# A raw weight block in tile 1's last products and 256-column halves in tile 0's, at the two boundaries of a one-core transformer layer

## Chip, cores and metric

The kernel runs on one core of one Trainium2 chip. The metric is the device time of one execution in microseconds (us). The engines are PE (TensorE, matrix products; PEld is its weight loading), DVE (VectorE), ACT (ScalarE), POOL (GpSimd) and SP (SyncE, which here only issues transfers).

## What is computed

One layer on 256 tokens of width 2048: a feed-forward block, a token mixer and a second feed-forward block, each fed by a layer norm modulated with a shift and a scale (adaLN), and each followed by a gated, scaled residual and another layer norm. All in float32.

```python
def _modulate(x, shift, scale):
    return _layernorm(x) * (1 + scale) + shift

def _swiglu(h, w_in, w_out):
    gate, up = jnp.split(h @ w_in, 2, axis=-1)
    return (jax.nn.silu(gate) * up) @ w_out

def _layer(x, c, w_ada, b_ada, ...):
    ada = (jax.nn.silu(c) @ w_ada + b_ada)[:, None, :]
    sh1, sc1, g1, sh2, sc2, g2, sh3, sc3, g3 = jnp.split(ada, N_ADA, axis=-1)
    h = _swiglu(_modulate(x, sh1, sc1), ffn1_w_in, ffn1_w_out)
    x = _layernorm(ALPHA * x + 0.5 * (1 + g1) * h, ln1_g, ln1_b)
    h = _token_mixer(_modulate(x, sh2, sc2), w_in, ..., w_out)
    x = _layernorm(ALPHA * x + (1 + g2) * h, ln2_g, ln2_b)
    h = _swiglu(_modulate(x, sh3, sc3), ffn2_w_in, ffn2_w_out)
    x = _layernorm(ALPHA * x + 0.5 * (1 + g3) * h, ln3_g, ln3_b)
    return x
```

The inner width of the feed-forward blocks is 5632, that of the mixer 2048.

## The kernel before

**Products.** The 256 tokens are two tiles of 128, called tile 0 and tile 1 (the index `a`). A float32 operand is split into a high part in the format fp32r and the low rest (`split`, line 131: ACT casts the high part, DVE subtracts). A product is then three PE instructions, high x high, high x low and low x high (`mm3`, line 359). Where the unsplit float32 values are multiplied instead (line 604), one product of 512 columns shows as two PE instructions.

**Weights.** `load_w` (line 348) loads 1 MB from SP's queue into one of three buffers `raw`; the parts go to six buffers `hi` and six `lo`. The adaLN weights `ar` stream beside this, 512 KB at a time, through two buffers `araw`. Each is multiplied by the conditioning and accumulated on DVE (lines 145 and 147). A call `npump()` after a block of weights asks for the next of them; `need(n)` asks for all up to a point.

**Output projections.** `out_proj` (line 389) runs three times: after the first feed-forward block, after the mixer and after the second feed-forward block. It goes over column groups of 1024, 512 and 512. In the last group a block of weights has 4 rows of 128 and 512 columns. The last three blocks (`nheld`) are held: their products are kept back and issued by `finish`, first all of tile 0 (36 PE instructions), then all of tile 1 (36). The block ahead of them, like all earlier ones, is multiplied for both tiles as it arrives (24 instructions).

**Boundaries.** `boundary` (line 509) follows the first and the second projection. On DVE its order is written out by hand: tile 0's `add_up` (gate, residual, statistics: lines 420, 422, 425), `row_std`, the affine step of the layer norm in parts (`ln_affine`, lines 472 and 477, with a square and its sum on ACT for each part, line 482), the statistics of the result (`ln_stats`, lines 488 to 503), then the normalised rows `n` (line 319 on DVE, 321 on ACT), which PE transposes (line 325). The first step of tile 1's `add_up` stands inside tile 0's `ln_stats`, its other two behind the first `n`. Once transposed and modulated, tile 0 is multiplied with three raw blocks of the next weights (`cols_1024`, line 604), and then tile 1. The third projection ends in `to_out` (line 568), which adds up, normalises and stores.

**Order.** Inside the boundary, DVE's instructions keep the order of the code. Otherwise a planner puts each engine's instructions in order; a buffer goes to whoever asked for it first in the code.

Of the kernel before, what the change touches and what calls it, by code (L numbers as in the profile page):

```python
# [15 lines left out]
P = 128  # L16
# [18 lines left out]
def layer_kernel(  # L35
# [312 lines left out]
    def load_w(src, nk, w, name):  # L348
# [3 lines left out]
        for q in range(nk // h):  # L352
# [3 lines left out]
            for kk in range(h):  # L356
                yield q * h + kk, hi[:, kk, :], lo[:, kk, :]

    def mm3(o, ah, al, bh, bl, start, stop):
        PE.matmul(o, ah, bh, start=start, stop=False)  # L360
        PE.matmul(o, ah, bl, start=False, stop=False)  # L361
        PE.matmul(o, al, bh, start=False, stop=stop)  # L362
# [25 lines left out]

    def out_proj(w, rows, nk, tag, npump, finish, before=None, turn=0, nheld=3):
        st = [stat_tile(f"{tag}{a}") for a in range(2)]  # L390
# [10 lines left out]
        for width in (1024, 512, 512):  # L401
# [3 lines left out]
            lastg = col + width == D  # L405
            held = []

            def products(a, args):
                ts_ = slice(a * P, (a + 1) * P)
                for k, hh, hl, hi, lo in args:  # L410
                    for b in range(nb):
                        mm3(ps[a, b], hh[:, ts_], hl[:, ts_], hi[:, b * 512:(b + 1) * 512],
                            lo[:, b * 512:(b + 1) * 512], k == turn, k == (turn - 1) % nk)


            def add_up(a, ps=ps, col=col, bs=range(nb)):
                for b in bs:
                    cs = slice(col + b * 512, col + (b + 1) * 512)
                    r = res[:, a, cs]
                    V.tensor_tensor(out=ps[a, b], in0=ps[a, b], in1=gate[:, cs], op=ALU.mult)  # L420
                    yield
                    V.scalar_tensor_tensor(out=r, in0=r, scalar=ALPHA, in1=ps[a, b],
                                           op0=ALU.mult, op1=ALU.add)
                    yield
                    V.bn_stats(st[a][:, col // 512 + b, :], r)
                    yield

            for i in range(nu):
                u = (i + turn // kn) % nu
                hs = []  # L430
                if before:
                    before(u * kn)
                for k in range(u * kn, u * kn + kn, 2):
                    hs += rows(k)
                for kk, hi, lo in load_w(w[u * kn * P:(u + 1) * kn * P, col:col + width], kn, width,
                                         f"{tag}o{col}_{u}"):
                    arg = (u * kn + kk, *hs[kk], hi, lo)
                    if lastg and i >= nu - nheld or not lastg and i == nu - 1:
                        held.append(arg)
                    else:  # L440
                        for a in range(2):
                            products(a, [arg])
                if not lastg and i == nu - 1:

                    late += [add_up(a, bs=(b,)) for b in range(nb) for a in range(2)]
                    products(0, held)
                    catch_up(2)
                    products(1, held)
                else:
                    catch_up(2)  # L450
                if not lastg or i < nu - 4:
                    npump()
            if lastg:
                catch_up(99)
                finish(lambda a: products(a, held), add_up, st)
            else:
# [11 lines left out]
    def ln_affine(a, rs, mv, lgb, sums, tag):  # L468
        for h in range(2):
# [4 lines left out]
            yield  # L474
        for i, (c0, c1) in enumerate(((0, 1024), (1024, 1536), (1536, 2048))):
            r = res[:, a, c0:c1]
            V.scalar_tensor_tensor(out=r, in0=r, scalar=rs, in1=lgb[1][:, c0:c1], op0=ALU.mult, op1=ALU.add,
                                   accum_out=sums[:, i:i + 1])
            if i == 0:
                V.tensor_scalar_mul(sums[:, 4:5], sums[:, 0:1], -2.0 / D)  # L480
            sq = npool.tile([P, 1024], F32, tag="sq", name=f"sq_{tag}{a}{i}")
# [4 lines left out]
    def ln_stats(out_, sums, tag):  # L486
# [4 lines left out]
        yield  # L491
        V.tensor_scalar(out=s[3], in0=s[1], scalar1=s[0], scalar2=1.0 / D, op0=ALU.subtract, op1=ALU.mult)
        yield
        V.tensor_scalar(out=s[2], in0=s[3], scalar1=s[3], scalar2=-1.0, op0=ALU.mult, op1=ALU.mult)
        yield
# [13 lines left out]
    def boundary(products, add_up, st, lgb, v, tag, xT, entry, nk):  # L509
# [3 lines left out]
        with tc.manual_schedule(engines={mybir.EngineType.DVE}):  # L513
            products(0)
            products(1)
            for _ in add_up(0):
                pass
# [5 lines left out]
            together(lns[0])  # L523
            up = add_up(1)
            next(up)
            together(lns[0])
# [4 lines left out]
            next(m0[1])  # L531
            next(up)
            next(up, 0)
            together(row_std(mv[1], rs[1], st[1], f"{tag}a1"))
# [33 lines left out]
    def to_out(products, add_up, st, lgb):  # L568
        mv, rs = ([small(n, t, f"{t}_last{a}") for a in range(2)] for n, t in ((2, "mv"), (1, "rs")))
        with tc.manual_schedule(engines={mybir.EngineType.DVE}):  # L570
            products(0)
            products(1)
            def first(a, j):
# [9 lines left out]
            for a in range(2):  # L583
                for _ in add_up(a):
                    pass
# [227 lines left out]

    out_proj(ffn1_w_out[0], h_rows, KF, "f1", at(R_OUT), finish1)
    xp, npool = ent["xp"], ent["np"]
# [385 lines left out]

    out_proj(w_out[0], y_rows, KD, "mx", step, finish2, before, 4, 3)
    xp, npool = ent["xp"], ent["np"]
# [115 lines left out]
```

## Time and profile before

| what | value |
|---|---|
| median of 3 runs | 1977.12 us (1975.76 to 1977.9) |
| the profiled execution's own time | 1974.53 us |
| its span, first to last instruction | 1972.8 us |
| mean granted PE clock | 0.991 |
| tile 0's add-up begins, boundary 1 and 2 | 778.70 and 1208.08 us |
| first transposition, boundary 1 and 2 | 792.03 and 1221.52 us |
| tile 1's add-up begins in `to_out` | 1960.09 us |

The profile is of one execution. Its lines give an engine, the line of the kernel, the operation, the tiles written and read, and times in us (a mean or the shortest, median and longest in ns). Idle time stands in brackets with what ended it. The profiled execution is 2.6 us under the median of the runs.

### The profile page before, as it was taken

The numbers are of one execution on the slowest core, as the hardware profiler recorded it, in microseconds if no ns is written. First come the engines' busy times: TensorE is split into PE (matmuls) and PEld (weight loads), VectorE is DVE, ScalarE is ACT, GpSimd is POOL, SyncE is SP. The second block draws the span as 40 slices with busy tenths as digits, with TensorE's granted clock in tenths as the row PEclk, the third lists the DMA queues.
The fourth block names the chain that finished last, engine by engine and source line by source line (L and its number), as shares of the span: only waits on it lengthen the run. The fifth ranks groups of instructions, "written<-read, shape, count | busy, mean of one in ns | idle before, by whom it ended". The sixth has DMA issues, their size and how long they took to land.

```text
span 1972.8 us, 32259 instructions
## 1 busy us (share of the span) xinstructions
PE 1899.0 (96%) x13057; PEld 1730.9 (88%) x13057; DVE 1494.4 (76%) x1878; ACT 962.5 (49%) x1394; POOL 5.7 (0%) x17
## 2 busy tenths in 40 slices
PE   3999999999999999999999998999999999999997
PEld 3999999999988887588899876898999999988886
DVE  7798888777778897678788689678757645555776
ACT  3644454443444555645655544655444444444553
POOL 0000000000000000000000000000000000000000
PEclk9999999999999999999999999999999999999998
DMA  9998878989989785489887875898858755665552
GB/s 332 337 331 312 300 242 288 311 293 305 304 298 324 262 303 195 140 304 307 257 294 261 281 263 179 259 309 298 266 193 276 257 193 193 227 200 192 192 192 85
DMA packets 301820, 510.89 MB, mean 259 GB/s; under 512 B 10818, under 2 KB 158690, under 8 KB 300648
## 3 DMA queue, kind: packets, MB, share of 16 engines
q1 hardware_dynamic: 300808, 505.70, 76.0%
q0 software_dynamic: 864, 3.15, 0.5%
q8 instruction: 102, 1.67, 0.3%
q14 instruction: 46, 0.38, 0.1%
HBM read 506.71 MB, written 2.10 MB: 258 GB/s over the span
## 4 chain that ended last, share of the span: by engine, by line
PE 77%; DVE 9%; DMA 8%; ACT 2%; issue 2%; DVEq 0%; SPq 0%; ACTq 0%
PE o_f L360 8%; PE o_f L362 8%; PE o_f L361 8%; PE gu_f L362 8%; PE gu_f L360 8%; PE gu_f L361 8%; DMA ar<-in_w_ada_dram 5%; PE s L362 3%; PE s L360 3%; PE s L361 3%; DVE acc L147 2%; PE fs L362 1%; PE fs L360 1%; PE fs L361 1%; PE fh L362 1%
## 5 line engine op out<-in xcount | busy, mean ns | idle before, releaser
L147 DVE SCALAR_TENSOR_TENSOR acc<-ar,csil,acc 128x1024 f32<-128x1024 f32 x242 | 307.9, 1273 | 109.5 <-DMA ar<-in_w_ada_dram 108.1
L360 PE MATMUL s<-xhi_f,hi_s 128*128 128x256 f32 x768 | 215.0, 280 | 0.7 <-ACT hi_s L132 0.6
L362 PE MATMUL s<-xhi_f,lo_s 128*128 128x256 f32 x768 | 214.3, 280 | 0.3 <-DVE lo_s L133 0.3
L361 PE MATMUL s<-xlo_f,hi_s 128*128 128x256 f32 x768 | 214.5, 279 | 0.0
L362 PE MATMUL gu_f<-xhi_f,lo_f2i 128*128 128x256 f32 x768 | 212.3, 276 | 0.0
L360 PE MATMUL gu_f<-xhi_f,hi_f2i 128*128 128x256 f32 x768 | 212.3, 276 | 0.0
L361 PE MATMUL gu_f<-xlo_f,hi_f2i 128*128 128x256 f32 x768 | 212.3, 276 | 0.0
L133 DVE TENSOR_TENSOR lo_f2i<-raw_f2i,hi_f2i 128x1024 fp32r<-128x1024 f32 x96 | 117.3, 1224 | 88.9 <-ACT hi_f2i L132 88.9
L360 PE MATMUL gu_f<-xhi_f,hi_f1i 128*128 128x256 f32 x640 | 177.1, 277 | 0.3 <-DVE hT L727 0.3
L362 PE MATMUL gu_f<-xhi_f,lo_f1i 128*128 128x256 f32 x640 | 177.0, 277 | 0.0
L361 PE MATMUL gu_f<-xlo_f,hi_f1i 128*128 128x256 f32 x640 | 176.9, 276 | 0.0
L132 ACT CAST hi_f2i<-raw_f2i 128x1024 fp32r<-128x1024 f32 x96 | 100.6, 1049 | 132.1 <-PE gu_f L361 115.7
L132 ACT CAST hh<-hT 128x512 fp32r<-128x512 f32 x130 | 80.1, 623 | 141.0 <-PE o_f L361 138.2
L360 PEld LDWEIGHTS s<-xhi_f,hi_s 128*128 128x128 f32 x768 | 146.2, 191 | 1.0 <-ACT hi_s L132 0.7
L362 PEld LDWEIGHTS s<-xhi_f,lo_s 128*128 128x128 f32 x768 | 145.8, 190 | 0.8 <-DVE lo_s L133 0.8
L361 PEld LDWEIGHTS s<-xlo_f,hi_s 128*128 128x128 f32 x768 | 146.3, 190 | 0.3 <-DVE xlo_f L309 0.3
L361 PEld LDWEIGHTS gu_f<-xlo_f,hi_f2i 128*128 128x128 f32 x768 | 144.3, 188 | 0.2
L360 PEld LDWEIGHTS gu_f<-xhi_f,hi_f2i 128*128 128x128 f32 x768 | 144.2, 188 | 0.2
L362 PEld LDWEIGHTS gu_f<-xhi_f,lo_f2i 128*128 128x128 f32 x768 | 144.2, 188 | 0.0
L132 ACT CAST hi_s<-raw_s 128x1024 fp32r<-128x1024 f32 x96 | 97.4, 1050 | 95.5 <-DMA raw_s<-in_ffn_w_in_dram 56.3
L133 DVE TENSOR_TENSOR lo_f2o<-raw_f2o,hi_f2o 128x1024 fp32r<-128x1024 f32 x88 | 107.8, 1225 | 44.9 <-ACT hi_f2o L132 44.8
L360 PE MATMUL o_f<-hi_f2o,hh 128*128 128x512 f32 x344 | 135.3, 393 | 0.0
(451 smaller groups left out, 5373.3 us busy)
## 6 DMA issues: line engine op xcount, KB each, us to landing
ar<-in_w_ada_dram SPq DMA_DIRECT2D x288, 512.0 KB, 5.6
raw_s<-in_ffn_w_in_dram SPq DMA_DIRECT2D x48, 1024.0 KB, 6.3
raw_f2i<-in_ffn_w_in_dram SPq DMA_DIRECT2D x48, 1024.0 KB, 5.1
raw_f1o<-in_ffn_w_out_dram SPq DMA_DIRECT2D x44, 1024.0 KB, 7.0
raw_f2o<-in_ffn_w_out_dram SPq DMA_DIRECT2D x44, 1024.0 KB, 5.1
raw_f1i<-in_ffn_w_in_dram SPq DMA_DIRECT2D x40, 1024.0 KB, 7.4
raw_mxo<-in_w_out_dram SPq DMA_DIRECT2D x16, 1024.0 KB, 5.6
raw_fh<-in_ffn_w_in_dram SPq DMA_DIRECT2D x16, 1024.0 KB, 6.8
```

The lines of the kernel that those rows point to most:

```text
L132: S.copy(hi, src)
L133: V.tensor_tensor(out=lo, in0=src, in1=hi.bitcast(F32), op=ALU.subtract)
L147: V.scalar_tensor_tensor(out=acc, in0=raw, scalar=csil[:, k:k + 1], in1=acc, op0=ALU.mult, op1=ALU.add)
L360: PE.matmul(o, ah, bh, start=start, stop=False)
L361: PE.matmul(o, ah, bl, start=False, stop=False)
L362: PE.matmul(o, al, bh, start=False, stop=stop)
```

## The change

- `load_kept` loads the block ahead of the held ones by two transfers of 512 KB into the two `araw` buffers, and splits each. It is used in the first and the second projection (`raw_row`). This block's products for tile 0 are issued as it arrives; those for tile 1 come at the head of tile 1's last products, as unsplit float32 values (`hT` or `yF` times the raw weights), four products of 512 columns.
- `products` can go by columns of a given width. Tile 0's held products go by 256 columns at all three places, tile 1's only in `to_out`. `add_up` can do the same: tile 0's at the boundaries, and both tiles' in `to_out`.
- The affine step's last parts are 512, 768 and 768 columns instead of 1024, 512 and 512. The estimate of the mean comes from the first part, so the constants of `ln_stats` change with it.
- At the boundaries, all of tile 1's `add_up` comes behind the first two `n`.

```diff
+    def load_kept(src, nk, w, name):
+        h = nk // 2
+        for q in range(2):
+            raw = ap.tile([P, h, w], F32, tag="araw", bufs=2, name=f"raw_{name}{q}")
+            SP.dma_start(raw, src[q * h * P:(q + 1) * h * P].rearrange("(k p) n -> p k n", p=P))
+            hi = wp.tile([P, h, w], F32R, tag="hi", bufs=6, name=f"hi_{name}{q}")
+            lo = wp.tile([P, h, w], F32R, tag="lo", bufs=6, name=f"lo_{name}{q}")
+            split(raw, hi, lo)
+            for kk in range(h):
+                yield q * h + kk, hi[:, kk, :], lo[:, kk, :], raw[:, kk, :]
...
-            def products(a, args):
+            def products(a, args, w=512):
                 ts_ = slice(a * P, (a + 1) * P)
-                for k, hh, hl, hi, lo in args:
-                    for b in range(nb):
-                        mm3(ps[a, b], hh[:, ts_], hl[:, ts_], hi[:, b * 512:(b + 1) * 512],
-                            lo[:, b * 512:(b + 1) * 512], k == turn, k == (turn - 1) % nk)
+                for c in range(0, 512, w):
+                    for k, hh, hl, hi, lo in args:
+                        for b in range(nb):
+                            bs = slice(b * 512 + c, b * 512 + c + w)
+                            mm3(ps[a, b][:, c:c + w], hh[:, ts_], hl[:, ts_], hi[:, bs], lo[:, bs],
+                                k == turn, k == (turn - 1) % nk and c + w == 512)
+
+            def last_products(a, w=512):
+                if a:
+                    for k, raw in kept:
+                        PE.matmul(ps[1, 0], raw_row(k)[:, P:], raw, start=k == turn, stop=False)
+                products(a, held, w)
...
+                keep = lastg and i == nu - nheld - 1 and raw_row
+                for kk, hi, lo, *raw in (load_kept if keep else load_w)(
+                        w[u * kn * P:(u + 1) * kn * P, col:col + width], kn, width, f"{tag}o{col}_{u}"):
                     arg = (u * kn + kk, *hs[kk], hi, lo)
-                    if lastg and i >= nu - nheld or not lastg and i == nu - 1:
+                    if keep:
+                        products(0, [arg])
+                        kept.append((u * kn + kk, raw[0]))
+                    elif lastg and i >= nu - nheld or not lastg and i == nu - 1:
                         held.append(arg)
...
-        for i, (c0, c1) in enumerate(((0, 1024), (1024, 1536), (1536, 2048))):
+        for i, (c0, c1) in enumerate(((0, 512), (512, 1280), (1280, 2048))):
...
-                V.tensor_scalar_mul(sums[:, 4:5], sums[:, 0:1], -2.0 / D)
+                V.tensor_scalar_mul(sums[:, 4:5], sums[:, 0:1], -4.0 / D)
...
-            products(0)
+            products(0, 256)
             products(1)
-            for _ in add_up(0):
+            for _ in add_up(0, w=256):
                 pass
...
             together(lns[0])
-            up = add_up(1)
-            next(up)
             together(lns[0])
...
             next(m0[0])
             next(m0[1])
-            next(up)
-            next(up, 0)
+            for _ in add_up(1):
+                pass
...
-            products(0)
-            products(1)
+            products(0, 256)
+            products(1, 256)
...
-                for _ in add_up(a):
+                for _ in add_up(a, w=256):
                     pass
...
-    out_proj(ffn1_w_out[0], h_rows, KF, "f1", at(R_OUT), finish1)
+    out_proj(ffn1_w_out[0], h_rows, KF, "f1", at(R_OUT), finish1, raw_row=lambda k: hT[:, k, :])
...
-    out_proj(w_out[0], y_rows, KD, "mx", step, finish2, before, 4, 3)
+    out_proj(w_out[0], y_rows, KD, "mx", step, finish2, before, 4, 3, lambda k: yF[:, k, :])
```

31 lines of the change are left out of this document (15 added, 16 removed).

## The prediction

> **What bounds the kernel now.** I read the page first: busy times, then the chain that ended last.
> ```profile
> PE 1899.0 (96%) x13057; PEld 1730.9 (88%) x13057; DVE 1494.4 (76%) x1878; ACT 962.5 (49%) x1394; POOL 5.7 (0%) x17
> ...
> PE 77%; DVE 9%; DMA 8%; ACT 2%; issue 2%; DVEq 0%; SPq 0%; ACTq 0%
> ```
> PE is busy for 96% of the span, so an edit pays only where PE idles or where its work shrinks. Of the places that this edit touches, two are such idles. I read the timeline there, engine by engine (columns: start us, length us, engine, line, operation, and in brackets the idle time before it with its releaser). Boundary 1:
> ```profile
> 778.70 0.70 DVE L420 TENSOR_TENSOR o_f<-o_f,gate 128x512 f32<-128x512 f32 x1 [4.97 <-PE o_f L362]
> ...
> 784.51 1.28 DVE L477 SCALAR_TENSOR_TENSOR res<-res,rs,lb 128x1024 f32<-128x1024 f32 x1 [0.42 <-ACT rs L264]
> ...
> 785.91 0.74 DVE L477 SCALAR_TENSOR_TENSOR res<-res,rs,lb 128x512 f32<-128x512 f32 x1
> 786.03 1.15 ACT L482 ACTIVATE sq<-res,sums 128x1024 f32<-128x1024 f32 x1 [1.55 <-DVE sums L480]
> 788.78 0.19 ACT L482 ACTIVATION_READ_ACCUMULATOR sq<-res,sums 128x1 f32 x1
> 788.26 0.69 DVE L420 TENSOR_TENSOR o_f<-o_f,gate 128x512 f32<-128x512 f32 x1
> 789.00 0.27 DVE L498 TENSOR_SCALAR sums<-sums 128x1 f32<-128x1 f32 x1
> 791.48 0.41 DVE L319 TENSOR_SCALAR n<-res,mr 128x256 f32<-128x256 f32 x1
> 792.03 1.09 PE L325 MATMUL tp<-ident,n 128*128 128x128 f32 x4 [5.13 <-DVE n L319]
> 804.63 1.09 ACT L321 ACTIVATE n<-res,mr 128x256 f32<-128x256 f32 x2 [2.58 <-DVE mr L503]
> 806.35 0.60 PE L325 MATMUL tp<-ident,n 128*128 128x128 f32 x4
> ```
> Tile 0's last product ends at 778.7. DVE then runs the layer norm, 12.8 us up to `n` at 791.48. PE works on tile 1's products meanwhile and then waits 5.13 us for the first transposition (792.03). Tile 1's own chain gives its `n` at 804.63 (the first of the pair is ready near 805.2), yet its transposition comes only at 806.35: there PE was late, by 1.1 us. Boundary 2 is the same code:
> ```profile
> 1208.08 0.70 DVE L420 TENSOR_TENSOR o_mx<-o_mx,gate 128x512 f32<-128x512 f32 x1 [0.83 <-PE o_mx L362]
> 1234.04 1.09 ACT L321 ACTIVATE n<-res,mr 128x256 f32<-128x256 f32 x2 [2.58 <-DVE mr L503]
> 1234.70 0.93 PE L325 MATMUL tp<-ident,n 128*128 128x128 f32 x4
> ```
> Here the second `n` is ready near 1234.6 and the transposition follows at once: the chain through DVE ends last, with PE just in time. So the end of each boundary is the start of tile 0's add-up plus a DVE chain of some 26.5 us, and at boundary 1 PE adds 1.1 us on top.
>
> **Why PE was late at boundary 1.** The last columns of this view by stretches are busy time, records, granted clock, DMA share and GB/s:
> ```profile
> 792.03:800.00 7.97, 7.84 (x16) 0.61 0.04 12
> 1221.50:1226.80 5.30, 5.16 (x13) 0.68 0.04 15
> 770.20:786.50 16.30, 16.30 (x72) 1.00 0.42 146
> 1680.00:1695.00 15.00, 15.00 (x135) 1.00 0.57 179
> ```
> After the 5.1 us of idle the granted clock was 0.61 over 7.97 us and 0.68 over 5.30 us: 3.1 and 1.7 us of PE time lost. Boundary 1 lost the more, and only there was PE behind the chain. The last two rows are prices at clock 1.00: 16.3/72 = 0.226 us for a product of 512 columns, 15.0/135 = 0.111 us for one of 256.
>
> **The change, part by part.** *The raw block.* Per boundary, 12 products of tile 1 leave the stretch ahead of tile 0's end: 12 x 0.226 = 2.7 us. Four float32 products come in after it, at the head of tile 1's. Their price is that of the raw products the kernel has:
> ```profile
> 1224.98 9.61 PE L604 MATMUL ge<-raw_gu,xf 128*128 128x512 f32 x22
> ```
> 22 instructions in 9.61 us, and there are two of them to one product of 512 columns: 0.87 us, 3.5 us for four. PE then ends tile 1 at 3.5 + 36 x 0.226 = 11.6 us after tile 0. DVE asks for that tile, and PE is wanted for the transposition, some 12.6 and 13 us after it: hidden in the idle. Without that cover each further us would cost one.
>
> *The halves of 256 columns.* PE pays nothing: 72 x 0.111 = 8.0 us against 36 x 0.226 = 8.1. A last product of 256 columns is shorter, 276 ns against the 0.39 us that the PE row further down shows, so tile 0 ends 0.1 us earlier.
> ```profile
> L362 PE MATMUL gu_f<-xhi_f,lo_f2i 128*128 128x256 f32 x768 | 212.3, 276 | 0.0
> ...
> L384 ACT ACTIVATE sg_f<-gu_f x44: 371/385/390, 340.6 to 1719.1; 128x256 f32<-128x256 f32 x44
>   PE gu_f L362: 26.0, 18
> 1444.31 0.41 DVE L1270 TENSOR_TENSOR hT<-hT,fs 128x256 f32<-128x256 f32 x1
> ```
> Whether DVE can add up the first half while PE fills the second is shown by L384. It reads the first 256 columns of a 512-column PSUM tile, which were complete when the gate half ended, one whole up half (16 x 2 x 3 x 0.111 = 10.7 us) earlier. It still waits for the last product into the other 256: 26.0 us in 18 of its 44 cases. So I take it that the first half waits for the second, and the split only costs: four DVE steps of 0.41 us for two of 0.70, +0.24 us at each add-up on the path. [...]
>
> The halves also want the last held block sooner: after 30 of 72 products, 3.3 us from the start, where 512 columns want it after 30 of 36, 6.8 us.
> ```profile
> 771.71 1.22 DVE L133 TENSOR_TENSOR lo_f1o<-raw_f1o,hi_f1o 128x1024 fp32r<-128x1024 f32 x1
> ```
> Its last low part is done at 772.9, 2.7 us after the held products began at 770.2, and the slot that it waits for will again come free as they begin: 3.3 us is just enough. I put 0.2 us of waiting (0 to 1.2: the upper end is one such subtraction more).
>
> *Squares and the moved add-up.* The first part of the affine step shrinks from 1024 to 512 columns (1.28 to 0.74 us), so ACT's three squares begin 0.5 us earlier and carry the same columns; the last ended at 788.97, and DVE's L498 at 789.00 waited for it. The second square of 768 waits a little for DVE, so -0.4 us. Tile 1's L420 sat in that wait (788.26, free); it now comes behind `n`, into tile 1's chain: +0.7 us (0.4 to 0.7, as ACT's root chain is then less crowded).
>
> *The slots of the raw blocks.* The raw block loads by two transfers of 512 KB into the two slots that the adaLN weights `ar` use, in place of one of 1 MB. On SP they go past the held loads, which gain a buffer by it; POOL's queue is not touched. Each must wait until an accumulation of the last `ar` blocks frees a slot (rows of DVE, SP, PE and ACT in the order of the argument):
> ```profile
> 740.09 0.37 SPq L169 DMA_DIRECT2D ar<-in_w_ada_dram  x1
> 769.85 0.75 DVE L145 TENSOR_SCALAR acc<-ar,csil 128x1024 f32<-128x1024 f32 x1
> ar<-in_w_ada_dram SPq DMA_DIRECT2D x1, 512.0 KB, 4.2
> 1190.58 1.28 DVE L147 SCALAR_TENSOR_TENSOR acc<-ar,csil,acc 128x1024 f32<-128x1024 f32 x1
> 1189.55 2.70 SPq L169 DMA_DIRECT2D ar<-in_w_ada_dram  x2
> ar<-in_w_ada_dram SPq DMA_DIRECT2D x3, 512.0 KB, 3.9
> 1194.11 1.22 DVE L133 TENSOR_TENSOR lo_mxo<-raw_mxo,hi_mxo 128x1024 fp32r<-128x1024 f32 x1
> 1199.56 0.39 PE L360 MATMUL o_mx<-hi_mxo,yh 128*128 128x512 f32 x1
> 1193.02 0.70 SPq L350 DMA_DIRECT2D raw_mxo<-in_w_out_dram  x1
> 1202.48 2.00 ACT L132 CAST hi_mxo<-raw_mxo 128x1024 fp32r<-128x1024 f32 x2 [6.56 <-DMA raw_mxo<-in_w_out_dram]
> ```
> At boundary 1 the slots are free by 740.1, when the next `ar` takes one, and the block is wanted 24 x 0.226 = 5.4 us ahead of the held products of 770.2: 24 us of cover. But the `ar` load that took that slot, and its step L145, were done ahead of the boundary; the load now waits for tile 1's first two raw products (2 x 0.87 = 1.7 us after tile 0's end), lands 4.2 us later, and L145's 0.75 us falls into the DVE chain, with all of tile 0's norm queued behind it and PE waiting for that. Bounds: 0.33 if it fits the 0.42 us idle at 784.51, 4.95 if DVE stands through the whole landing. I take 0.75, since the planner puts it where it expects the data.
>
> At boundary 2 the cover is gone. The last accumulation ends at 1191.9, so the second transfer starts then (the first at 1189.55) and lands, with 3.9 us, at 1195.8. Cast 1.0 us (half of the ACT pair), subtraction 1.22 us, and five products of 0.226 still to run: the held products begin at 1199.2. Before, they began at 1199.56. So 0.3 us of the 2.7 is left. Bounds: all 2.7 if the accumulations come 2.5 us sooner, and a delay of 5.1 us if the load takes as long as the row of 1193.02, whose cast could start only at 1202.48, 9.4 us on.
>
> *The end.* Behind the last product of all stands the add-up of tile 1: +0.24 - 0.1 = +0.1 us. Tile 0's part stays under tile 1's products.
>
> **The sum.** Boundary 1: -2.7 - 0.1 + 0.2 + 0.24 - 0.4 + 0.7 + 0.75, and the 1.1 us by which PE was late goes, since its idle is now under 3 us and its clock matters less: -2.4 us. Boundary 2: -0.3 - 0.1 + 0.24 - 0.4 + 0.7 = +0.1. End: +0.1. Together -2.2 us: 1974.53 to 1972.3 for the profiled execution (span 1972.8), and from the median of 1977.12, 2.6 us above it, to 1974.9. A measurement of this kernel tells from no change about 0.2%, 4 us; this lies below.
>
> **The rivals.**
> 1. *The halves do overlap.* Then after the last product only two steps of 0.41 us stand where 1.40 us stood: -0.58 instead of +0.24, at three places: 2.5 us more, 1972.4. For it: the code asks for it. Against: L384's 18 waits. Chance 0.11.
> 2. *The clock stays full and PE is what ends each boundary.* Both losses come back, 3.1 + 1.7 = 4.8 us more: 1970.1. For it: the idle shrinks from 5.1 to 1 to 2 us. Against: tile 1's `n` leaves PE only 1.1 and 0.1 us to gain. [...] Chance 0.11.
> 3. *The raw block is there in time at boundary 2.* 2.4 us more: 1972.5. It needs the `ar` stream to run 2.5 us ahead of its rows. Chance 0.14.
> 4. *It lands late there.* 5.1 us of delay instead of 0.3 of gain: 1980.3; past a landing of 1198 the whole change loses. Chance 0.10.
> 5. *Slower: L145 keeps its place ahead of tile 0's add-up in DVE's order.* Then the norm starts 1.7 + 4.2 + 0.75 = 6.7 us after tile 0's end, less the 0.75 already counted: +5.9 us, 1980.8. It decides as soon as L145 stands ahead of L420. For it: it is asked for earlier in the code, and DVE is held in order only inside the boundary. Against: the planner places a step where its data is expected. Chance 0.06.
>
> **How the numbers follow.** The forecast has 0.45, another order by the planner 0.03. The range runs from rival 2 to rival 4: 1970.0 to 1980.5. Faster by over 0.2% (under 1973.2): 0.07 of the forecast's 0.45, 0.07 of rival 1, 0.10 of 2, 0.08 of 3, 0.01 of the rest: 0.33. Slower (over 1981.1): 0.02, then 0.04 of 4, 0.04 of 5, 0.01: 0.11. Within: 0.56.
>
> **What the profile after would show.** Right: tile 0's first L420-type step about 2.7 us earlier at boundary 1, and after all 72 products; PE's idle there under 3 us and clock near 1.00; L145 of `ar` inside the boundary; PE waiting for the raw block's parts in front of boundary 2. Wrong: an add-up that starts while the second half still runs, no PE wait at boundary 2, or L145 ahead of the add-up.

## Result and profile after

The changed kernel takes 1990.23 us (median of 8 runs, 1984.2 to 1995.83) against 1978.05 us of the kernel before on the same chip (8 runs, 1974.38 to 1983.75). The ratio is 1.0059 (95% interval 1.0038 to 1.0079): slower by some 12 us, where 2.2 us less were forecast. The profiled execution of after took 1992.33 us (span 1990.6, clock 0.988). The page, engines first, then the shares of the chain that ended last:
```profile
PE 1907.7 (96%) x13193; PEld 1739.5 (87%) x13193; DVE 1496.2 (75%) x1886; ACT 962.1 (48%) x1394; POOL 5.7 (0%) x17
...
PE 67%; DMA 14%; DVE 12%; ACT 4%; issue 3%; SPq 0%; DVEq 0%; ACTq 0%
```
DMA holds 14% of that chain where it held 8%: something now waits for transfers.

Single executions differ, so one rerun of the old program (e8 below, "twin") stands beside both in the table of stages. All times are in us, from the traces.

| stretch | before | twin | after |
|---|---|---|---|
| span | 1972.8 | 1981.2 | 1990.6 |
| second stage begins | 316.3 | 318.3 | 321.2 |
| boundary 1: raw block's first product to tile 0's add-up | 14.46 | 14.45 | 13.06 |
| boundary 1: the same to tile 1's first transposition | 42.1 | 41.1 | 41.7 |
| boundary 2: first `o_mx` product to first `ge` product | 105.0 | 106.6 | 113.4 |
| `fh` stage (first `fh` product to first `gf` product) | 92.4 | 92.9 | 96.7 |

"Raw block" means the block ahead of the held ones, in every kernel. The start of the second stage wanders by itself. Boundary 1 is even, boundary 2 lost 7 to 8 us, and the `fh` stage, which the change does not touch, 4. Against the mean of before and twin that is 0.1 + 7.6 + 4.0 = 11.7 us, about the loss that the medians show (12.2).

Boundary 1 of after in the timeline (start, length, engine, line, operation; in brackets the idle time before and its releaser):
```profile
775.11 1.02 PE L434 MATMUL o_f<-raw_f1o,hT 128*128 128x512 f32 x2
...
781.78 0.43 DVE L444 TENSOR_TENSOR o_f<-o_f,gate 128x256 f32<-128x256 f32 x1 [4.10 <-PE o_f L374]
...
786.71 0.75 DVE L145 TENSOR_SCALAR acc<-ar,csil 128x1024 f32<-128x1024 f32 x1 [0.33 <-DMA ar<-in_w_ada_dram]
...
795.70 0.66 PE L325 MATMUL tp<-ident,n 128*128 128x128 f32 x4 [3.11 <-DVE n L319]
...
799.09 0.46 ACT L335 ACTIVATE xf<-tp,scsh 128x128 f32<-128x128 f32 x1 [1.63 <-PE tp L325]
...
802.56 0.75 DVE L504 SCALAR_TENSOR_TENSOR res<-res,rs,lb 128x512 f32<-128x512 f32 x1 [0.97 <-ACT rs L264]
...
810.41 0.82 PE L325 MATMUL tp<-ident,n 128*128 128x128 f32 x3 [1.25 <-ACT n L321]
```
Two of the eight PE instructions of the raw products (L434) run at 775.11, among tile 0's. The adaLN step L145 stands inside the norm, as forecast. Tile 1's norm then waits 0.97 us for its `rs` (0.32 at the same step of before): ACT stood 1.63 us for a transposition (799.09) with the root chain of `rs` queued behind it.

Boundary 2:
```profile
1194.36 2.16 SPq L364 DMA_DIRECT2D raw_mxo<-in_w_out_dram  x2
...
1201.77 1.04 ACT L132 CAST hi_mxo<-raw_mxo 128x1024 fp32r<-128x1024 f32 x1 [4.98 <-DMA raw_mxo<-in_w_out_dram]
...
1202.86 0.66 PE L372 MATMUL o_mx<-hi_mxo,yhi 128*128 128x512 f32 x1 [4.54 <-ACT hi_mxo L132]
1203.32 3.44 PE L434 MATMUL o_mx<-raw_mxo,yF 128*128 128x512 f32 x4
...
1219.78 0.43 DVE L444 TENSOR_TENSOR o_mx<-o_mx,gate 128x256 f32<-128x256 f32 x1 [6.56 <-PE o_mx L374]
...
1233.20 1.09 PE L325 MATMUL tp<-ident,n 128*128 128x128 f32 x4 [5.37 <-DVE n L319]
```
The raw block's loads go out from 1194.36, its first high part is cast at 1201.77, and PE stands 4.54 us for it. At once four raw instructions run (3.44 us at a granted clock of 0.55, 0.86 us each; e9 below takes 3.60 us for eight, 0.45 each), ahead of all held products of tile 0. The wait for `n` (5.37 us) is there as before.

One profiled execution (e10) ran at a granted clock of 0.56 throughout and is used for nothing; its kernel ran again as e15.

### The profile page after: what moved, and what is told of

Same layout as the page of the kernel before. It is cut to its first block, busy times and chain, and to the rows that moved or that the text cites. A ratio compares the mean times of both kernels' runs of the same rounds, so it can differ in the third digit from the quotient of the medians.

```text
span 1990.6 us, 32543 instructions
## 1 busy us (share of the span) xinstructions
PE 1907.7 (96%) x13193; PEld 1739.5 (87%) x13193; DVE 1496.2 (75%) x1886; ACT 962.1 (48%) x1394; POOL 5.7 (0%) x17
## 4 chain that ended last, share of the span: by engine, by line
PE 67%; DMA 14%; DVE 12%; ACT 4%; issue 3%; SPq 0%; DVEq 0%; ACTq 0%
DMA ar<-in_w_ada_dram 9%; PE o_f L372 8%; PE o_f L374 8%; PE o_f L373 8%; PE gu_f L374 7%; PE gu_f L372 7%; PE gu_f L373 7%; DVE acc L147 3%; DMA raw_s<-in_ffn_w_in_dram 2%; DVE lo_s L133 2%; PE s L372 2%; PE s L374 2%; PE s L373 2%; PE fs L372 1%; PE fs L374 1%
## 5 line engine op out<-in xcount | busy, mean ns | idle before, releaser
L372 PE MATMUL o_f<-hi_f2o,hh 128*128 128x512 f32 (+1 forms) x368 | 139.4, 379 | 0.0
```

## Experiments

Each ratio is to the kernel before on the same chip, from five rounds, with its 95% interval.

**One part at a time (e1 to e4).** e1 takes the raw block away at boundary 2:
```diff
-    out_proj(w_out[0], y_rows, KD, "mx", step, finish2, before, 4, 3, lambda k: yF[:, k, :])
+    out_proj(w_out[0], y_rows, KD, "mx", step, finish2, before, 4, 3)
```


> The changed kernel, with the raw block at boundary 1 alone; boundary 2 keeps the 256-column products, the halved add-up, the squares and the moved add-up. Theory A (late block): boundary 2 lost 8.4 us because the raw block waits for the adaLN slots and PE for the block. Then PE has no wait of over 1 us ahead of the held products at boundary 2, the clock stays at 1.00 there, and boundary 2 is within 1.5 us of the kernel before; the time falls by about 8 us, to some 1982. If the 4.4 us lost in the fh stage (its adaLN loads shifted by the raw block) have the same cause, they go too, and the time is some 1978. Theory B (the loss comes from the 256-column products and the reordered norm, the late block is only seen beside it): boundary 2 still loses over 5 us and the time stays at 1987 to 1992.

Measured: 1.0028 (1.0012 to 1.0043). Boundary 2's stage takes 108.3 us, 5 less than in after, and 1.7 to 3.3 more than in before and its twin. So theory A has the larger part, and not all: PE still waits 1.7 and 0.9 us, now for the high and low parts of the last *held* block. The `fh` stage stays long (95.2).

e2 has the raw block at boundary 2 and nothing else:
```diff
+    out_proj(w_out[0], y_rows, KD, "mx", step, finish2, before, 4, 3, lambda k: yF[:, k, :])
```


> The kernel before, with nothing but the raw block at boundary 2. Theory A: all of boundary 2's loss is here: PE waits 4 to 5 us for the block's high part, runs at half clock after it, and has its raw products ahead of tile 0's end; boundary 2 is 7 to 9 us longer, and the fh stage some 4 us if that hangs on the shifted adaLN loads: 1985 to 1990. Theory B: boundary 2 is at most 2 us longer, 1978 to 1980. The prediction as it was: boundary 2 0.3 us shorter, 1977.7.

Measured: 1.0033 (1.0016 to 1.0049). PE waits 4.2 us for the high part, four of the eight raw instructions run ahead of tile 0's, boundary 2 takes 110.5 us. For boundary 2 theory A holds in kind; in size the stage is 4 to 5.5 us longer than in before and twin, not 7 to 9. The `fh` stage (91.7) does not hang on it.

e3 has the halves alone:
```diff
-            products(0)
+            products(0, 256)
...
-            for _ in add_up(0):
+            for _ in add_up(0, w=256):
```


> The kernel before, with only the 256-column products and the halved add-up (both boundaries and the end). The prediction: add-up begins after all 72 products, nothing overlaps, about +0.1 us at each of three places: 1978.4 (no difference). Rival 1 of the prediction (the first half is added up while PE fills the second): 2.5 us faster, 1975.5, and an add-up that begins before the last product. Third theory: the 256-column products cost PE more than the 512-column ones per column, or the earlier wanted held block makes PE wait: 1 to 3 us slower, with waits among tile 0's products.

Measured: 1.0017 (1.0003 to 1.0031): the third theory. Its boundary 2, ACT, PE and DVE:
```profile
1200.71 1.99 ACT L132 CAST hi_mxo<-raw_mxo 128x1024 fp32r<-128x1024 f32 x2 [5.35 <-DMA raw_mxo<-in_w_out_dram]
...
1203.07 0.39 PE L373 MATMUL o_mx<-lo_mxo,yhi 128*128 128x256 f32 x1 [0.87 <-DVE lo_mxo L133]
...
1209.38 0.43 DVE L444 TENSOR_TENSOR o_mx<-o_mx,gate 128x256 f32<-128x256 f32 x1 [3.90 <-PE o_mx L374]
```
By halves PE is at the last held block after 24 of 72 products. There it waits 0.87 us for that block's low part. At boundary 1 nothing waits, but tile 0's end comes after 14.83 us instead of 14.45, and `n` 13.17 us after the add-up instead of 12.78. Nothing overlaps. These waits and steps are not the whole of the 3.4 us, though: boundary 2's stage takes 106.6 us as in the twin, and the `fh` stage 95.7.

e4 has the squares and the moved add-up alone:
```diff
-        for i, (c0, c1) in enumerate(((0, 1024), (1024, 1536), (1536, 2048))):
+        for i, (c0, c1) in enumerate(((0, 512), (512, 1280), (1280, 2048))):
...
-            up = add_up(1)
-            next(up)
```


> The kernel before, with only the new cut of the squares and the first step of tile 1's add-up moved behind tile 0's first n. The prediction: tile 0's n 0.4 us earlier, tile 1's n 0.3 us later, so +0.3 us at each boundary: 1978.6 (no difference). Rival: tile 1's chain is not what ends the boundary, so the earlier n counts: -0.4 us at each, 1977.2; the traces tell it by the start of the two transpositions against tile 0's first add-up step.

Measured: 1.0004 (0.9994 to 1.0014). `n` comes 12.40 us after the add-up (12.78 before): -0.38, as forecast. Tile 1's first transposition at boundary 2 comes 26.82 us after the add-up (26.62 in before, 27.01 in the twin), so the squares and the moved step together cost next to nothing there, where +0.3 was forecast. What each of the two does to tile 1's chain was not measured alone.

**Order and slots in the changed kernel (e5, e6).** e5 holds PE to the order of the code:
```diff
+            with tc.manual_schedule(engines={mybir.EngineType.PE}):
-            products(0, 256)
-            products(1)
+                products(0, 256)
+                products(1)
```


> The changed kernel, with PE too held to the order of the code for the last products at the boundaries: all of tile 0's, then tile 1's raw ones, then the rest. Theory A (the planner puts part of the raw float32 products and a product of tile 1 among tile 0's, so they delay tile 0's end): at boundary 1 the add-up begins 1.9 us earlier after the stage's start (238.2 against 240.1 us) and the raw products come behind tile 0's; at boundary 2, where they partly fill a wait, 1 to 3 us earlier; 1986 to 1988. Theory B (they only fill time in which PE waits anyway): add-up at 240.1 us again and the time unchanged, 1989 to 1991. If PE then idles longer ahead of the transposition and runs at half clock for longer: above 1991.

Measured: 1.0048 (1.0032 to 1.0065), so not told apart from after. Boundary 1's add-up comes after 12.67 us (13.06): the raw products among tile 0's cost 0.4 us, not 1.9. Counted from the stage's start, as theory A has it, the add-up comes no sooner (240.4 us, 240.0 in after). Theory A is wrong in size, and the time agrees with theory B.

e6 loads boundary 2's raw block into the ring:
```diff
+        if name[:2] == "mx":
+            big.append(wp.tile([P, nk, w], F32, tag="raw", bufs=3, name=f"raw_{name}"))
+            SP.dma_start(big[0], src.rearrange("(k p) n -> p k n", p=P))
```


> The changed kernel, with boundary 2's raw block loaded as before in one transfer of 1 MB into the ring of three buffers instead of the adaLN slots, and kept there until its raw products are done. Theory A1 (only this block was late): no PE wait for the high part ahead of the held products; the add-up at boundary 2 begins 88 to 89 us after the stage's start (98.8 in the changed kernel, 90.4 in the kernel before): about 10 us less, 1980. Theory A2 (behind it the last held block is wanted too soon by the 256-column order, as in the run with the halves alone, 91.6 us, and the run without boundary 2's raw block, 93.7 us): the wait moves to the last held block and the add-up begins at 91 to 94 us: 1983 to 1986. Rival: the ring is short of a buffer, the next stage's weights come late, and what is won is lost in waits of PE for them behind the boundary.

Measured: 1.0053 (1.0034 to 1.0071), boundary 2's stage 108.6 us. The block is in time; PE begins the held products 78.4 us into the stage and then waits for the last held block, whose high part is cast at 85.1. All raw products and some of tile 1's fill that wait; add-up at 94.0: A2.

**Boundary 1 alone, and the twin (e7, e8).** e7 has the raw block at boundary 1 and nothing else:
```diff
+    out_proj(ffn1_w_out[0], h_rows, KF, "f1", at(R_OUT), finish1, raw_row=lambda k: hT[:, k, :])
```


> The kernel before, with nothing but the raw block at boundary 1. The prediction's terms: tile 0's add-up 2.7 us earlier (238.5 us after the stage's start against 241.2), the adaLN step of 0.75 us inside the norm, the first transposition 2 us earlier, PE's lateness of 1.1 us gone: the second transposition 2 to 3 us earlier and 1975.5 to 1977. Theory A of the order (raw products go among tile 0's): the add-up only 0.8 to 1.2 us earlier, with nearly all of it lost to the adaLN step: no difference, 1978 to 1979.

Measured: 0.9998 (0.9985 to 1.0011). DVE, then PE:
```profile
776.86 0.70 DVE L444 TENSOR_TENSOR o_f<-o_f,gate 128x512 f32<-128x512 f32 x1 [2.92 <-PE o_f L374]
...
782.22 0.76 DVE L145 TENSOR_SCALAR acc<-ar,csil 128x1024 f32<-128x1024 f32 x1
...
788.53 0.70 DVE L444 TENSOR_TENSOR o_f<-o_f,gate 128x512 f32<-128x512 f32 x1 [1.83 <-PE o_f L374]
```
```profile
792.16 0.63 PE L325 MATMUL tp<-ident,n 128*128 128x128 f32 x4 [3.67 <-DVE n L319]
```
The add-up comes after 11.88 us: 2.58 us sooner. But the step of tile 1's add-up inside tile 0's statistics (788.53) now waits 1.83 us for tile 1's last product, which the raw products push back. `n` comes 14.74 us after the add-up, and the gain is gone.

e8 is the old program in the new text:
```diff
-            products(0, 256)
+            products(0)
```
(and likewise for every other part)

> The program of the kernel before in the text of the changed one, with every part of the change switched off: how far two runs of one program lie apart, in the time and in the start of the stages. No difference in time (ratio within 0.15% of 1). The profiled execution of before began its second stage at 316.3 us and those of the others at 317.8 to 321.2: if that is chance, this run lies among the others; if it is the change, at 316.3 again. The wait of PE in the last part of the feed-forward product (2.5 to 3.6 us in the three runs that have the 256-column products) does not show.

Measured: 1.0005 (0.9991 to 1.002); second stage at 318.3, `fh` stage 92.9.

**Boundary 1 without halves (e9, e10, e15).** e9 is e7 with squares, moved add-up and e5's order:
```diff
+            with tc.manual_schedule(engines={mybir.EngineType.PE}):
+                products(0)
+                products(1)
```


> The kernel before with the raw block at boundary 1 alone, the new squares, the moved add-up, and PE held to the order of the code for the last products; 512 columns everywhere. Counted from the raw block's first product for tile 0 (14.5 us to the add-up in the kernel before and its twin, 13.1 in the changed one): the add-up after 11.9 us, as in the run with the raw block alone, the raw products behind tile 0's. Theory A (the gain is real and was eaten behind it): unlike in that run DVE does not stand for tile 1's last product, so tile 0's n comes 12.5 to 13.2 us after the add-up (14.7 there); but tile 1's root chain on ACT still stands behind the second transposition pair, so the second transposition comes 28 to 28.5 us after the add-up (26.5 to 27.7 without a raw block) and 1 to 2 us are left: 1976.5 to 1978, which the times cannot tell from no change. Rival: all of it is lost, second transposition 29 us or more after the add-up, 1978.5 to 1980.

Measured: 0.9995 (0.9979 to 1.001). PE:
```profile
780.23 3.60 PE L434 MATMUL o_f<-raw_f1o,hT 128*128 128x512 f32 x8
...
793.68 0.66 PE L325 MATMUL tp<-ident,n 128*128 128x128 f32 x4 [1.61 <-DVE n L319]
...
807.36 0.82 PE L325 MATMUL tp<-ident,n 128*128 128x128 f32 x3 [1.59 <-ACT n L321]
```
Add-up (780.43) after 11.88 us, the raw products behind it for 3.60 us, and tile 1's transposition 38.8 us after the raw block's first product, 2.3 and 3.3 us sooner than in twin and before. Theory A holds, with somewhat more left than the 1 to 2 us that it expected; the times do not show it.

e10 and e15 are e9 with boundary 1's raw block in the ring (e6's edit there):
```diff
+        if name[:2] == "f1":
+            big.append(wp.tile([P, nk, w], F32, tag="raw", bufs=3, name=f"raw_{name}"))
+            SP.dma_start(big[0], src.rearrange("(k p) n -> p k n", p=P))
```

> The run before this one, with boundary 1's raw block as one transfer of 1 MB in the ring of three buffers instead of the two adaLN slots. Theory: no adaLN step waits for a slot, so none falls into tile 0's norm, whose n comes 12.4 us after the add-up (0.2 to 0.7 us less). Rival: the ring lacks a buffer until the raw products are done, a held block or the mixer's first weights come late, and PE waits for one of them by more than 1 us: slower than the run before it by as much.

> The same kernel as the run with boundary 1's raw block in the ring, which has no usable trace. Theory: boundary 1 alone is shorter, by the 2.3 to 3.3 us of the run with the adaLN slots and up to 0.7 us more, because no adaLN step falls into tile 0's norm; all other stages are as in the kernel before; ratio 0.997 to 0.999. Rival: the gain lies partly in another stage (the adaLN stream is not pushed back by the raw block, so a wait for it goes somewhere): a stage other than boundary 1 is shorter by over 1.5 us than in the kernel before and its twin.

Measured: 0.9976 (0.9961 to 0.9992) and 0.9975 (0.9961 to 0.999): faster than both kernels, by some 5 us. DVE, then PE in e15:
```profile
775.67 0.70 DVE L451 TENSOR_TENSOR o_f<-o_f,gate 128x512 f32<-128x512 f32 x1 [2.39 <-PE o_f L381]
...
788.15 0.41 DVE L319 TENSOR_SCALAR n<-res,mr 128x256 f32<-128x256 f32 x1
```
```profile
788.62 0.55 PE L325 MATMUL tp<-ident,n 128*128 128x128 f32 x3 [1.31 <-DVE n L319]
```
```profile
802.30 0.93 PE L325 MATMUL tp<-ident,n 128*128 128x128 f32 x4 [1.59 <-ACT n L321]
```
No adaLN step stands in the norm, `n` comes 12.48 us after the add-up, and tile 1's transposition 38.5 us after the raw block's first product. That is 2.9 us less than the mean of before, twin and e2 (41.4; one program up to there). The whole stage, first `o_f` to first `mo` product, takes 251.2 us where before and twin take 255.8 and 257.2. So the rest of the gain in this execution lies in the same stage, ahead of the raw block (its first product comes 225.4 us into the stage, 226.8 and 228.2 there); why is not known, and that start wanders in the other runs too. No later stage is clearly shorter.

**Is the landing the limit at boundary 2? (e11)** The raw block at boundary 2 in the ring, 512 columns, squares, moved add-up and order (e6's and e9's edits together):
```diff
-    out_proj(ffn1_w_out[0], h_rows, KF, "f1", at(R_OUT), finish1, raw_row=lambda k: hT[:, k, :])
+    out_proj(ffn1_w_out[0], h_rows, KF, "f1", at(R_OUT), finish1)
...
+        if name[:2] == "mx":
+            big.append(wp.tile([P, nk, w], F32, tag="raw", bufs=3, name=f"raw_{name}"))
```

> The kernel before with the raw block at boundary 2 alone, as one transfer into the ring of three buffers, with the new squares, the moved add-up and PE's order held; 512 columns. Theory (the last held block's landing sets the end of tile 0 at boundary 2, whatever is taken away ahead of it: its high part was cast 83 to 85 us after the stage's start in every run so far): PE begins the held products 2.7 us earlier, at 79 us, and then waits about 2 us for the last held block's parts; add-up at 90 to 91.5 us (90.4 and 92.0 in the kernel before and its twin): nothing gained, 1978 to 1980. Rival (PE's products set the end): add-up at 87.5 to 89.5 us, no wait, 2.5 us faster.

Measured: 1.0035 (1.002 to 1.005). SP, ACT, PE and DVE:
```profile
1200.66 0.37 SPq L350 DMA_DIRECT2D raw_mxo<-in_w_out_dram  x1
```
```profile
1208.64 1.99 ACT L132 CAST hi_mxo<-raw_mxo 128x1024 fp32r<-128x1024 f32 x2 [8.37 <-DMA raw_mxo<-in_w_out_dram]
```
```profile
1209.73 0.80 PE L379 MATMUL o_mx<-hi_mxo,yhi 128*128 128x512 f32 x1 [3.37 <-ACT hi_mxo L132]
```
The rival did not come. The theory is right in kind: PE waits 3.37 us for the last held block, so its landing does set tile 0's end. In size it is wrong: the load went out 79.5 us into the stage instead of 75.3, because the raw block keeps a buffer of the ring; so the add-up comes at 94.9, worse than before. What a fourth buffer would bring was not tried.

**The halves, undone and mended (e13, e14).** e13 is the changed kernel with 512 columns everywhere:
```diff
-            products(0, 256)
+            products(0)
...
-            for _ in add_up(0, w=256):
+            for _ in add_up(0):
```


> The changed kernel with 512 columns everywhere: only the halves are undone. Theory (halves draw the raw products in): at boundary 1 the raw products come behind tile 0's, the add-up 11.9 us after the raw block's first product (13.1 in the changed kernel), the second transposition 38.8 to 40 us after it (41.7); at boundary 2 the block is as late as before and costs 5 to 6 us; no wait for the last held block's low part; 5 to 7 us less than the changed kernel, 1983 to 1985. Rival (the halves only cost their own two steps of DVE and 0.1 us of PE at each place): boundary 1 within 1 us of the changed kernel, 1988 to 1990.

Measured: 1.002 (1.0007 to 1.0033), about two thirds of the loss gone. Boundary 1: add-up after 11.87 us, raw products behind it without any order being held, transposition after 39.0 us. Boundary 2: 110.4 us. `fh`: 91.9 us. The theory holds. Against after that is 2.7 us less at boundary 1, 3.0 at boundary 2 and 4.8 in the `fh` stage.

e14 is e3 with PSUM tiles of their own for tile 0's halves (e12, the same idea, gave no result):
```diff
+            ph = lastg and tag != "f2" and mm_tile(f"o_{tag}h")
+            def part(a, b, c, w, ps=ps, ph=ph):
+                return ph[:, :w] if ph and not a and c else ps[a, b][:, c:c + w]
```


> The run with the halves alone, but tile 0's two halves in PSUM tiles of their own at the two boundaries (there tile 0's products of the last column group go by 256 columns throughout). Theory: what held the first half's add-up was the shared tile; with its own, its two steps run some 4 us ahead of tile 0's last product, only two steps of 0.43 us and the statistics stand behind it, and tile 0's n comes about 12.3 us after the second half's first step (13.2 us after the first step in the run with the halves alone). Rival: the first half still waits for the last product. The times will hardly tell: 1979 to 1982, since the last held block is still wanted early at boundary 2 (PE waits 1 to 3 us for it).

Measured: 1.0022 (1.0007 to 1.0038). DVE:
```profile
779.63 0.43 DVE L450 TENSOR_TENSOR o_f<-o_f,gate 128x256 f32<-128x256 f32 x1 [1.15 <-PE o_f L374]
780.10 0.42 DVE L452 SCALAR_TENSOR_TENSOR res<-res,o_f 128x256 f32<-128x256 f32 x1
783.95 0.43 DVE L450 TENSOR_TENSOR o_f1h<-o_f1h,gate 128x256 f32<-128x256 f32 x1 [3.43 <-PE o_f1h L374]
```
The first half is added up 4.3 us ahead of the second. `n` comes 12.25 us after the second half's first step. So it was the shared tile that held it: with two tiles DVE works on the first half from 779.63 to 780.52 while PE is still at the second, for whose last product DVE then waits 3.43 us. Counted from tile 0's last product, `n` comes 0.9 us sooner than in e3, which is about what the halves cost at boundary 1 (0.38 and 0.39 us).

**The `fh` stage (e16, e17).** The first block of weights that is asked for within this stage (its load goes out 0.6 to 1.0 us into it) is the "second block" of the expectations below. ACT's cast of it, the waits of PE (us in total, times, longest) and the DMA queues in one microsecond (packets, MB, share of 16 engines) in after:
```profile
1273.12 1.05 ACT L132 CAST hi_fh<-raw_fh 128x1024 fp32r<-128x1024 f32 x1 [2.35 <-DMA raw_fh<-in_ffn_w_in_dram]
```
```profile
PE bc L160 <- ACT ahi L132: 3.6, 1, 3.6
```
```profile
q8 instruction: 1, 0.02, 7.2%
```
The same cast in e13:
```profile
1266.08 1.05 ACT L132 CAST hi_fh<-raw_fh 128x1024 fp32r<-128x1024 f32 x1 [1.02 <-DMA raw_fh<-in_ffn_w_in_dram]
```
In all six traces with halves (after, e1, e3, e5, e6, e14) this cast waits 2.3 to 2.5 us and comes 8.0 to 8.4 us into the stage; in the nine without, 1.0 us and 6.7 to 7.0. Issue times are alike. In the six, a packet of 16 KB on the queue for instructions falls 2 to 4 us into the stage, within that transfer; in the others 8 to 12 us. The kernel of before fetched 102 such packets (1.67 MB) for 2 x 13,057 PE instructions, and after 103 for 2 x 13,193, which comes to 256 each, an estimate from these counts; the halves add 72 products and 72 weight loads ahead of the stage. The packet takes 7.2% of 16 engines for 1 us, 1.15 us of one. e16 shifts PE's code without halves, e17 the halves' code back:
```diff
+                    if j == 1 and i < 6 and not h and not b and k == 4 * j:
+                        for _ in range(12):
+                            PE.matmul(ps[:, :T], hi[:, fs], xT[0][:, k, :], start=True, stop=True)
```
(in e17 seven times 8)

> The program of the kernel before with 72 more products on PE in the first stage (they are overwritten by the products after them and change no value), so that PE's code ahead of the fh stage is as long as with the halves at both boundaries. Theory (a packet of PE's code, 256 instructions, delays the transfer that it falls into): the packet comes 2 to 4 us into the fh stage, the cast of the second block waits 2.3 to 2.5 us for its transfer and comes 8 to 8.4 us into the stage (6.7 to 7.0 in the kernel before), and the stage takes 93 to 97 us (92.3 and 93.0). Rival (the halves do it in another way): packet at 2 to 4 us, but the cast at 6.7 to 7.0 us.

> The run with the halves alone, with 56 more products on PE in the first stage (overwritten likewise): with the halves' 72 that is 128 products and their 128 weight loads, one whole packet of code, so that the packets fall as in the kernel before. Theory: the packet comes 8 to 12 us into the fh stage, the cast of the second block at 6.7 to 7.0 us, the stage takes 91.7 to 93.5 us (95.8 in the run with the halves alone). Rival: the cast at 8 to 8.4 us and the stage 94 to 97 us, as in the runs with the halves.

Measured, one execution each: e17 has the packet at 9 to 10 us, the cast at 6.9, the stage at 92.4 us. e16 has the packet at 2 to 3 us, the cast at 7.5, but the stage at 91.8 us. So the cast's delay goes and comes with the packet, by half in e16. The stage's loss does not: of the seven traces with an early packet, four have a long stage (after 96.7, e3 and e14 95.7, e1 95.2), and e5 (92.6), e6 (93.2) and e16 do not. (e17's time is no shorter for it: its boundary 2 takes 110.7 us, 4 more than in e3.)

What makes the stage long is PE's wait for `ahi`, a part of the adaLN row that PE multiplies in it, 80 to 84 us into the stage. The same wait in before and in e5, and the granted clock (third figure from the end) in the 10 us that follow it in after and in e5:
```profile
PE bc L160 <- ACT ahi L132: 0.5, 1, 0.5
```
```profile
PE bc L160 <- ACT ahi L132: 0.8, 1, 0.8
```
```profile
1348.46:1358.46 10.00, 9.96 (x69) 9.53 (x70) 9.39 (x15) 3.59 (x7) 0.00 (x0) 0.83 0.85 272
```
```profile
1348.90:1358.90 10.00, 9.46 (x78) 9.18 (x79) 9.26 (x15) 4.40 (x8) 0.00 (x0) 1.00 0.89 291
```
The wait is 3.6, 3.4, 3.0 and 2.5 us in after, e3, e14 and e1. In after the clock then is 0.50 from 1349.8 to 1353.2 us, which costs 1.7 us. The longest product of `fh` takes 420 ns there and 415 ns in e1. In all others the wait is at most 1.7 us (e7); the clock over the 10 us after it is 1.00 in before and e5, and no product of `fh` takes over 371 ns in before, e2, e4, e6, e7, e9, e11, e16 and e17. In after the longer wait (3.64 against 0.5 for `ahi` and 0.5 for its low part in before) and the clock make 2.6 + 1.7 = 4.3 us, all that the stage is longer than in before. The delayed cast may have a part in the late row; why the row is late in these four and not in e5, e6 and e16 is open.

## Why the prediction was wrong

| term, per boundary | forecast | measured |
|---|---|---|
| 12 products of tile 1 go | -2.7 | boundary 1: -2.58 (e7, e9, e13) |
| halves on PE | -0.1 | +0.38 (e3) |
| last held block wanted sooner | +0.2, at boundary 2 nothing | boundary 2: 0.9 (e3), 2.5 (e1) |
| add-up in halves | +0.24 | +0.39 (e3) |
| squares | -0.4 | -0.38 at tile 0's `n` (e4) |
| moved add-up | +0.7 | with the squares, boundary 2: within 0.2 of before and twin (e4) |
| adaLN step in the norm | +0.75 | 0.75, and 0.33 of waiting (after) |
| four raw products | 3.5, hidden | 3.60 (e9); partly not hidden |
| raw block late at boundary 2 | -0.3 in all | wait of 4.54, raw products ahead of tile 0's |

**What held.** Boundary 1 without halves gains 2.3 us (e13: 39.0 against 41.4), forecast 2.4. There the mechanism was right: tile 0's end sooner, raw products in PE's idle, the norm's chain behind. It needs the moved add-up (e7), which the prediction had only as a cost. That the two sizes agree so well is partly luck: the forecast's sum also holds 1.1 us of PE's lateness, which is no term of the change (below), and the halves' 0.34; without both it comes to 1.65.

**Step that failed: "The halves of 256 columns ... PE pays nothing".** Undoing them brings the ratio from 1.0059 to 1.002, with the largest part in the `fh` stage (e13). At the boundaries three things were missed. First, at boundary 1 a product of 256 columns steps by 0.120 us (e3) and one of 512 by 0.229 (before), so 72 take 8.64 us and 36 take 8.25; the prediction's 0.111 was a row of another stage, and its 0.226 divides a window by every record that touches it. Second, "after 30 of 72 products ... just enough" was read off boundary 1's last held block, and the sum of boundary 2 has no such term. At boundary 2 the quoted cast of 1202.48 is that very block, 2.9 us after the held products began at 1199.56, with its low parts to follow; PE by halves needs it after 24 x 0.119 = 2.9 us. Third, the planner's order: with halves it puts two of the eight raw instructions among tile 0's at boundary 1 (after, e1, e6), without them not (e7, e13); e5 prices that at 0.4 us. And PE idles longer ahead of the first transposition (3.11 us against 1.57 in e13); what that does to the clock stands below.

**Step that failed: "lands, with 3.9 us, at 1195.8".** The slots came free late, as forecast (second load 1196.15 in after, whose stage began 3.3 us later). But from issue to cast the two loads took 7.4 and 6.9 us (1194.36 to 1201.77, 1196.15 to 1203.05), behind a held block's 1 MB, where 3.9 us were counted. Alone, this block makes boundary 2's stage 4.7 us longer (e2). It was rival 4, given 0.10. Its wait (4.54, and 3.7 to 5.9 in e2, e5 and e13) was sized well (5.1); what it left out is that the raw products then come ahead of tile 0's, at a clock of 0.55 (after). From the end of the products ahead of the block to the add-up it is 21.5 us where it was 13.8.

**A term read from one execution.** The 1.1 us by which "PE was late" at boundary 1 is in before and not in its twin: the second transposition comes 27.65 and 26.64 us after the add-up. It comes and goes (e3 has 27.70), and is no term that the change takes away. That an idle of under 3 us leaves the clock near 1.00, as the forecast has it, is not shown either: after 1.57 us it was 0.72 in e13, after 1.61 us 1.00 in e9.

**Not thought of:** the `fh` stage, behind the change in time and with more code ahead of it. The sum has no term for it, and it holds 4.0 of the 11.7 us; which part of the change makes its adaLN row late is open.

**The other rivals.** Rival 1 did not come; e14 shows that the shared tile is why. Rival 2: with halves the clock did not stay full; without them at boundary 1 it did in e9 and e15 (1.00) and did not in e13 (0.72), and in e9 still the chain, not PE, ended the boundary (1.59 us of waiting for `n` at 807.36). Rival 3 is refuted by the 4.54 us. Rival 5 did not come.

## What to carry over

Cutting the last products by columns needs *all* the weights in the first half: look up when the last block lands before any gain is counted, at every place where it is done. A block that is moved to other buffers has to land earlier than the one it replaces; the date is set by who frees those buffers. And where a planner orders an engine, work meant for its idle time may be put earlier, as the raw products were: look where it went, or hold the order.

## What the runs showed of the chip

**The clock can fall after short waits.** Granted clock (third figure from the end) in the stretch that follows PE's wait for `n`, in after, e13 and e9:
```profile
795.70:800.00 4.30, 3.97 (x10) 2.08 (x11) 4.09 (x10) 2.23 (x8) 0.53 (x1) 0.63 0.38 126
```
```profile
791.67:796.00 4.33, 4.00 (x11) 2.17 (x12) 4.12 (x10) 2.97 (x10) 0.53 (x1) 0.72 0.33 121
```
```profile
793.68:798.00 4.32, 3.94 (x13) 1.87 (x14) 4.11 (x10) 3.20 (x11) 0.53 (x1) 1.00 0.37 121
```
After waits of 3.11, 1.57 and 1.61 us it was 0.63, 0.72 and 1.00. So the clock fell behind a wait of 1.57 us, and behind one of 1.61 us it did not: the wait's length alone is not the cause, and what sets e13 and e9 apart is open. In after it fell only some 1 us after the wait's end (1.00 from 795.70 to 796.50, 0.85 to 797.00, 0.50 to 800.00). In the `fh` stage a wait of 1.7 us (e7) was not followed by a fall that its products show (371 ns at most). In after the fall makes the second pair of transpositions late (the raw products ahead of it take 1.95 us, 1.12 in e9), and ACT's wait of 1.63 us (799.09) with it; in e9 that wait is 0.60 us.

**One packet of code can delay a transfer of 1 MB**, as far as e16 and e17 bear it out: the cast that waits for it comes about 0.6 us (e16) to 1.3 us (the runs with halves) later. That this makes the stage longer is not shown.
